# A small tile allotted 160 bytes more: the SBUF offset of every phase pool in a two-block transformer kernel

## The chip, the cores and the metric

The kernel runs on one core of one Trainium2 chip. The metric is the device time of one execution in microseconds; the runs shown are the median of three. One further execution was taken by the hardware profiler, and all views below are of that one.

## What is computed

Two transformer blocks on 256 tokens of width 2048, float32 throughout, one after the other. The first has a hybrid mixer (dilated attention, forgetting attention, gated linear attention), cross attention to 256 memory rows and a gated feed-forward with a short convolution; the second has a sparse attention, a gated delta rule, merge gates and a squared-ReLU feed-forward. Nearly all the work is in the products with the weights:

```python
def first_block(x, mem, ...):
    mem_n = rms_norm(mem, mem_norm)
    x = x + hybrid_mixer(rms_norm(x, norm_mix[l]), w_in[l], ..., w_out[l])
    x = x + memory_cross_attention(rms_norm(x, norm_cross[l]), mem_n, w_cq[l], w_ckv[l], w_co[l])
    x = x + conv_ffn(rms_norm(x, norm_ffn[l]), w_up[l], conv_w[l], conv_b[l], w_down[l])
    return rms_norm(x, norm_final)

def hybrid_layer(x, ...):                      # the second block
    proj = rms_norm_2(x, ln1_w) @ w_in
    ...
    x = x + (g_a * (o_a @ w_pa) + g_b * (o_b @ w_pb)) @ w_o
    h = rms_norm_2(x, ln2_w)
    return x + jnp.square(jax.nn.relu(h @ w_up)) @ w_down
```

## The kernel before

**Products.** A float32 product is made of three products of rounded parts. `chunk` (L327) brings 128x1024 weights from HBM by one transfer on SP's queue into a `raw` tile (four buffers), ScalarE rounds them into `hi`, VectorE takes the difference into `lo` (three buffers each); these tiles are in the pool "weights". Activations are kept the same way: a tile of 128x512 holds the rounded 256 columns and, behind them, the 256 columns of the rest. Such a tile is called `kt` where it comes from the pool "slots" (`new_kt`), `hk` where it comes from the pools "hidden1" and "hidden2" of the two feed-forwards, and `mkt` where it comes from the pool "late".

**Two forms.** `gemm_ws` (output tiles `ps_ws`, and `ps_pab` from `merged`) loads weights into TensorE's array and streams activations: each pair is 512 columns of `kt` over `hi` and 256 columns over `lo`. `gemm_as` (output tiles `ps_as`) loads 128 columns of an activation tile and streams 512 columns of weights, three matmuls a piece:

```python
def mm_as(o, kt, t, h, l, start, stop):
    xh, xl = kt[:, t * 128:t * 128 + 128], kt[:, 256 + t * 128:256 + t * 128 + 128]
    fill(o, xh, h, start, False)
    fill(o, xh, l, False, False)
    fill(o, xl, h, False, stop)
```

In the trace's names `ps_as<-hi,hk` is a matmul that streams `hi` over a loaded part of `hk`. All four down products of each feed-forward, and the product with `w_o` (from `mkt`), are of this form with tiles of the phase pools; `w_cv`, `w_v`, `w_out` and `w_co` are of this form with `kt` tiles of "slots". The rest of the large products are of the other form and stream `kt` tiles of "slots".

**Order.** A tile framework's scheduler lays down every engine's queue when the program is built, and allots SBUF. The long-lived pools come first, in the order const, weights, slots, norms, tiny; behind them are the pools of a phase, which `open_pools` opens and closes: "wide1", "held1", "work1" (mixer and cross attention), "hidden1", "work2" (first feed-forward), "gates" with "delta", then "wide2" and "heads", then "late" inside it (second block), "hidden2", "work4" (second feed-forward). The size of "tiny" thus sets where all of them begin.

**Places in SBUF** (byte offset in a partition, as the built program has them):

| tiles | pool | before | mod 512 |
|---|---|---|---|
| `raw`, `hi`, `lo` | weights | 24448 to 65408 | 384 |
| `kt` and other slots | slots | 67456 to 141184 | 384 |
| `pe` | tiny | 148064 | 96 |
| first phase tile | "wide1", "hidden1", "gates", "hidden2" | 149216 | 224 |
| `hk` | hidden1, hidden2 | from 149216, 2048 apart | 224 |
| `mkt` | late | from 171744, 2048 apart | 224 |
| tiles of "delta" behind the first padded tile | delta | from 175904 | 288 |

Of the kernel before, what the change touches and what calls it, by code (L numbers as in the profile page):

```python
# [225 lines left out]
def hybrid_blocks(ctx: ExitStack, tc: tile.TileContext, A: dict, out: bass.AP):  # L226
# [35 lines left out]
    def tiny(name, n, bufs=None):  # L262
        return tp.tile([128, n], F32, name=name, tag=name, bufs=bufs)
# [1056 lines left out]
    bias2 = []  # L1320
    for _ in bias_tiles(dtab2, bias2):
        pass
    pe = tiny("pe", 64, bufs=1)
    SP.dma_start(pe, A["pe"])
    w2c = wide("w2c", [128, 4, 128])
    SP.dma_start(w2c, A["cw2_2"].rearrange("p (a j) -> p a j", a=4))
# [275 lines left out]
```

## Time and profile before

| | |
|---|---|
| median of 3 runs | 2800.02 us (2799.59 to 2800.89) |
| profiled execution, device time | 2799.51 us |
| its span, first to last instruction | 2797.7 us |
| TensorE (PE) busy | 2765.9 us, 99% |
| weight loads into the array (PEld) | 2362.4 us, 84% |
| VectorE (DVE), ScalarE (ACT), GpSimd (POOL) busy | 65%, 49%, 6% |
| mean granted TensorE clock | 0.999 |

PE's busy time counts overlapping matmuls once, and a matmul's end is modelled, so a busy PE is not one at its peak. How fast the stream of matmuls runs is read from the starts of its rows in the timeline: a start belongs to the matmul itself, and the distance from one to the next is what one matmul costs when nothing is waited for. Rows of the timeline put neighbours of the same kind together (x2).

### The profile page before, as it was taken

The page shows a single profiled execution, that of the slowest core. Times are in us where ns is not written, and L with a number is a line of the kernel's source. Part 1 is how long each engine was busy: PE and PEld are TensorE (multiplying, and loading weights), DVE is VectorE, ACT ScalarE, POOL GpSimd, SP SyncE. Part 2 cuts the span into 40 slices and gives each one's busy share as a digit, 9 for nine tenths or more (in the row PEclk, how much of TensorE's full clock was granted, in tenths as well). Part 3 has the DMA queues.
Part 4 walks back from the last instruction along what each step waited for, and adds up shares of the span by engine and source line. Part 5 has one row for each costly group of instructions (what it writes and reads, how often), then busy time and mean ns, then how long its engine had stood idle before and what let it go on. Part 6 is the DMA issues. An engine that isn't in the chain of part 4 may idle for free.

```text
span 2797.7 us, 39304 instructions
## 1 busy us (share of the span) xinstructions
PE 2765.9 (99%) x14848; PEld 2362.4 (84%) x14848; DVE 1822.7 (65%) x2794; ACT 1379.1 (49%) x2230; POOL 169.4 (6%) x261
## 2 busy tenths in 40 slices
PE   7999999999999999999999999999999999999998
PEld 5988888888888888888889888888888888888887
DVE  7575675677764677657877767776656455565564
ACT  4545554544443444445555555555455344454453
POOL 5000000000000000000111010000100000000001
PEclk9999999999999999999999999999999999999999
DMA  6655446455555555565544448556666666666664
GB/s 214 184 173 176 144 146 203 159 187 192 185 185 187 188 188 184 182 209 184 179 151 149 152 143 255 171 151 185 188 202 192 185 191 188 188 190 188 189 188 158
DMA packets 148838, 507.28 MB, mean 181 GB/s; under 512 B 17036, under 2 KB 21672, under 8 KB 148648
## 3 DMA queue, kind: packets, MB, share of 16 engines
q1 hardware_dynamic: 148592, 504.74, 56.9%
q8 instruction: 116, 1.90, 0.3%
q14 instruction: 74, 0.61, 0.1%
q10 hardware_dynamic: 56, 0.04, 0.0%
HBM read 500.48 MB, written 4.23 MB: 180 GB/s over the span
## 4 chain that ended last, share of the span: by engine, by line
PE 96%; DVE 1%; ACT 1%; POOL 1%; DMA 1%; issue 0%; POOLq 0%; DVEq 0%; SPq 0%; ACTq 0%
PE ps_ws L272 51%; PE ps_as L272 34%; PE ps_pab L272 3%; PE ps_s L272 1%; PE ps_o L272 1%; PE ps_h L272 1%; PE ps_t L442 1%; PE ps_no L272 0%; PE ps_z L272 0%; PE ps_lv L272 0%; POOL mgate L1516 0%; DVE lo L337 0%; PE ps_y L272 0%; ACT hi L336 0%; DVE kt L404 0%
## 5 line engine op out<-in xcount | busy, mean ns | idle before, releaser
L337 DVE TENSOR_TENSOR lo<-raw,hi 128x1024 fp32r<-128x1024 f32 (+3 forms) x941 | 1144.7, 1218 | 785.2 <-ACT hi L336 777.8
L336 ACT CAST hi<-raw 128x1024 fp32r<-128x1024 f32 (+3 forms) x941 | 972.5, 1035 | 1051.9 <-PE ps_as L272 505.7
L272 PE MATMUL ps_ws<-kt,hi 128*128 128x512 f32 x4128 | 1466.0, 397 | 15.7 <-DVE kt L404 15.7
L272 PE MATMUL ps_ws<-kt,lo 128*128 128x256 f32 x4128 | 1173.3, 284 | 0.4 <-DVE lo L337 0.4
L272 PEld LDWEIGHTS ps_ws<-kt,hi 128*128 128x128 f32 x4128 | 778.3, 189 | 193.2 <-DVE kt L404 17.3
L272 PEld LDWEIGHTS ps_ws<-kt,lo 128*128 128x128 f32 x4128 | 784.0, 190 | 4.0 <-issue 2.6
L272 PE MATMUL ps_as<-hi,hk 128*128 128x512 f32 x1712 | 540.8, 396 | 0.0
L272 PEld LDWEIGHTS ps_as<-hi,hk 128*128 128x128 f32 x1712 | 322.5, 188 | 78.3
L272 PE MATMUL ps_as<-lo,hk 128*128 128x512 f32 x856 | 339.8, 397 | 0.0
L272 PE MATMUL ps_as<-hi,kt 128*128 128x512 f32 (+2 forms) x1024 | 295.2, 368 | 1.0 <-ACT hi L336 1.0
L272 PEld LDWEIGHTS ps_as<-hi,kt 128*128 128x128 f32 x1024 | 186.4, 188 | 26.6 <-ACT hi L336 1.4
L272 PEld LDWEIGHTS ps_as<-lo,hk 128*128 128x128 f32 x856 | 161.2, 188 | 38.8
L272 PE MATMUL ps_as<-lo,kt 128*128 128x512 f32 (+2 forms) x512 | 188.2, 368 | 0.9 <-DVE lo L337 0.9
L378 ACT COPY half<-ps_ws 128x256 f32<-128x256 f32 x258 | 95.0, 372 | 165.3 <-PE ps_ws L272 162.8
L379 DVE TENSOR_TENSOR half<-ps_ws,half 128x256 f32<-128x256 f32 x258 | 107.9, 421 | 63.6 <-ACT half L378 63.4
L272 PEld LDWEIGHTS ps_as<-lo,kt 128*128 128x128 f32 x512 | 96.3, 188 | 14.2 <-DVE lo L337 2.2
L272 PE MATMUL ps_pab<-kt,hi 128*128 128x512 f32 x256 | 91.3, 398 | 0.0
L272 PE MATMUL ps_as<-hi,mkt 128*128 128x512 f32 x256 | 82.1, 399 | 0.3 <-ACT hi L336 0.3
L272 PE MATMUL ps_pab<-kt,lo 128*128 128x256 f32 x256 | 72.9, 285 | 0.0
L272 PEld LDWEIGHTS ps_as<-hi,mkt 128*128 128x128 f32 x256 | 48.2, 188 | 12.1 <-issue 0.8
L272 PEld LDWEIGHTS ps_pab<-kt,hi 128*128 128x128 f32 x256 | 48.1, 188 | 11.1 <-DVE kt L401 0.2
L272 PE MATMUL ps_as<-lo,mkt 128*128 128x512 f32 x128 | 50.9, 398 | 0.3 <-DVE lo L337 0.3
(384 smaller groups left out, 1842.7 us busy)
## 6 DMA issues: line engine op xcount, KB each, us to landing
raw<-in_w_up SPq DMA_DIRECT2D x300, 512.0 KB, 3.6
raw<-in_w_dd SPq DMA_DIRECT2D x128, 512.0 KB, 3.7
raw<-in_w_dn SPq DMA_DIRECT2D x84, 512.0 KB, 4.3
raw<-in_w_m SPq DMA_DIRECT2D x64, 512.0 KB, 3.6
raw<-in_w_g SPq DMA_DIRECT2D x48, 512.0 KB, 3.3
raw<-in_w_qk SPq DMA_DIRECT2D x40, 512.0 KB, 3.3
raw<-in_w_v SPq DMA_DIRECT2D x32, 512.0 KB, 3.4
raw<-in_w_out SPq DMA_DIRECT2D x32, 512.0 KB, 3.3
```

What stands on the lines that cost most here:

```text
L272: return PE.matmul(o, l, r, start=start, stop=stop)
L336: ACT.copy(hi[:, a:b], raw[:, a:b])
L337: DVE.tensor_sub(lo[:, a:b], raw[:, a:b], hi[:, a:b])
L378: ACT.copy(s, ps[:, 256:512])
L379: DVE.tensor_tensor(s, ps[:, 0:256], s, op=ADD)
L442: PE.transpose(ps[:, t * 128:t * 128 + 128], x[:, c * 128:c * 128 + 128], ident)
```

## The change

The tile `pe`, which holds 64 float32 values a partition, is allotted 104 and used by its first 64: 416 bytes in place of 256. It is the tile before `kcc` and `H` in the pool "tiny", so these and every pool behind begin 160 bytes later: the first phase tile is at 149376 in place of 149216, which is 384 mod 512 in place of 224; `hk` and `mkt` are at 384 mod 512, the tiles of "delta" at 448. Weights, slots and norms stay where they are. On all five engines the queues hold the same instructions in the same order, with the same waits. A blank line is added ahead of L1323, so that lines behind it are one higher.

```diff
@@ -1320,7 +1320,8 @@
     bias2 = []
     for _ in bias_tiles(dtab2, bias2):
         pass
-    pe = tiny("pe", 64, bufs=1)
+
+    pe = tiny("pe", 104, bufs=1)[:, 0:64]
     SP.dma_start(pe, A["pe"])
```

## Rows read from the trace of the kernel before

**Rows 1.** The page: busy time, share, instructions; granted clock in 40 slices.

```profile
PE 2765.9 (99%) x14848; PEld 2362.4 (84%) x14848; DVE 1822.7 (65%) x2794; ACT 1379.1 (49%) x2230; POOL 169.4 (6%) x261
...
PEclk9999999999999999999999999999999999999999
```

**Rows 2.** The page: the chain that ended last, by engine.

```profile
PE 96%; DVE 1%; ACT 1%; POOL 1%; DMA 1%; issue 0%; POOLq 0%; DVEq 0%; SPq 0%; ACTq 0%
```

**Rows 3.** The page's groups: line, engine, operation, tiles, shape, count, busy us, mean ns.

```profile
L272 PE MATMUL ps_as<-hi,hk 128*128 128x512 f32 x1712 | 540.8, 396 | 0.0
...
L272 PE MATMUL ps_as<-lo,hk 128*128 128x512 f32 x856 | 339.8, 397 | 0.0
...
L272 PE MATMUL ps_as<-hi,mkt 128*128 128x512 f32 x256 | 82.1, 399 | 0.3 <-ACT hi L336 0.3
...
L272 PE MATMUL ps_as<-lo,mkt 128*128 128x512 f32 x128 | 50.9, 398 | 0.3 <-DVE lo L337 0.3
```

**Rows 4.** Timeline of PE, `hk` loaded: start us, duration us, instruction, count.

```profile
2169.82 0.39 PE L272 MATMUL ps_as<-lo,hk 128*128 128x512 f32 x1
...
2209.88 0.39 PE L272 MATMUL ps_as<-lo,hk 128*128 128x512 f32 x1
```

**Rows 5.** Timeline of PE, the same form with `kt` loaded.

```profile
212.07 0.39 PE L272 MATMUL ps_as<-lo,kt 128*128 128x512 f32 x1
...
251.51 0.39 PE L272 MATMUL ps_as<-lo,kt 128*128 128x512 f32 x1
```

**Rows 6.** Timeline of PE, the same form with `mkt` loaded.

```profile
2004.90 0.40 PE L272 MATMUL ps_as<-lo,mkt 128*128 128x512 f32 x1
...
2026.69 0.40 PE L272 MATMUL ps_as<-lo,mkt 128*128 128x512 f32 x1
```

**Rows 7.** Windows: stretch; busy us of PE, PEld, DVE, ACT, POOL; PEclk, DMA, GB/s.

```profile
212.00:252.00 40.00, 40.00 (x179) 33.11 (x178) 18.82 (x17) 17.81 (x22) 0.00 (x0) 1.00 0.56 194
2170.00:2210.00 40.00, 40.00 (x172) 32.14 (x172) 20.02 (x19) 14.87 (x15) 0.00 (x0) 1.00 0.61 188
```

**Rows 8.** Timeline of PE: `kt` loaded, just behind transposes that interrupt the stream.

```profile
454.19 0.60 PE L442 MATMUL ps_t<-cst,xs 128*128 128x128 f32 x4
...
454.87 0.40 PE L272 MATMUL ps_as<-lo,kt 128*128 128x512 f32 x1
...
456.96 0.39 PE L272 MATMUL ps_as<-lo,kt 128*128 128x512 f32 x1
...
457.64 0.39 PE L272 MATMUL ps_as<-lo,kt 128*128 128x512 f32 x1
```

**Rows 9.** Timeline of PE, pairs of the other form, second feed-forward.

```profile
2689.71 0.39 PE L272 MATMUL ps_ws<-kt,hi 128*128 128x512 f32 x1
...
2699.07 0.39 PE L272 MATMUL ps_ws<-kt,hi 128*128 128x512 f32 x1
```

**Rows 10.** Timeline of PE, the same pairs in the first feed-forward.

```profile
684.92 0.81 PE L272 MATMUL ps_tab<-ohr,tab 128*8 128x384 f32 x2
...
686.11 0.40 PE L272 MATMUL ps_ws<-kt,hi 128*128 128x512 f32 x1
...
693.88 0.40 PE L272 MATMUL ps_ws<-kt,hi 128*128 128x512 f32 x1
```

**Rows 11.** Groups of PE, 685.6 to 1171.2 us (first feed-forward).

```profile
L272 PE MATMUL ps_ws<-kt,hi 128*128 128x512 f32 x1024 | 362.0, 399 | 0.0
```

**Rows 12.** Groups of PE, 2073 to 2797 us (second feed-forward).

```profile
L272 PE MATMUL ps_ws<-kt,hi 128*128 128x512 f32 x1024 | 355.4, 391 | 0.0
```

**Rows 13.** Line L401, DVE: duration ns min/median/max, first and last start, forms.

```profile
L401 DVE TENSOR_TENSOR hk<-h,hk x64: 415/418/421, 2088.3 to 2704.7; 128x256 fp32r<-128x256 f32 x64
...
L401 DVE TENSOR_TENSOR kt<-gtmp,kt x8: 418/423/426, 1438.3 to 1676.9; 128x256 fp32r<-128x256 f32 x8
```

**Rows 14.** Groups by form: attention scores from work tiles, and from slots.

```profile
L272 PE MATMUL ps_s<-kpair,qpair 128*128 128x256 f32 x40 | 11.9, 379 | 0.0
...
L272 PE MATMUL ps_s<-ksw,nq 128*128 128x256 f32 x32 | 9.6, 380 | 0.0
```

## The prediction, made before the changed kernel ran

> **What bounds the kernel now.** I read the page's first part first: TensorE is busy for 2765.9 of 2797.7 us and its clock is granted in full, the 2.4 GHz level, in every slice [rows 1]. Then the chain of what ended last: 96% of it is TensorE's own [rows 2]. So there is hardly a wait to take away, and a change pays only if it alters how fast TensorE's stream of matmuls runs. The change removes, adds and moves no instruction; it moves tiles. The question is therefore whether a matmul's time depends on where its operands lie, and the trace can answer that, since it holds the same instruction with operands at different offsets.
>
> The form to look at is the one that loads part of an activation tile and streams 512 columns of weights. The streamed operand, `hi` or `lo`, always lies at 384 mod 512. The loaded one lies at 384 where it is a `kt` tile and at 224 where it is an `hk` or `mkt` tile. The busy column can't tell the rate, for matmuls overlap and each is shown for some 397 ns [rows 3]; the starts can:
>
> - `kt` loaded, 384: from 212.07 to 251.51 us there are 58 pieces of three matmuls, 39.44 us / 174 = 226.7 ns each [rows 5].
> - `hk` loaded, 224: from 2169.82 to 2209.88 us there are 57 pieces, 40.06 us / 171 = 234.3 ns each [rows 4].
> - `mkt` loaded, 224: from 2004.90 to 2026.69 us there are 31 pieces, 21.79 us / 93 = 234.3 ns each [rows 6].
>
> Nothing waits in these stretches. Side by side, equal windows of 40 us hold 179 matmuls with `kt` and 172 with `hk`, and what else goes on is much alike: VectorE busy 18.8 and 20.0 us, ScalarE 17.8 and 14.9 us, DMA 194 and 188 GB/s, clock 1.00 in both [rows 7]. The stretch with less ScalarE work and less DMA traffic is the slower one, so neither explains it. What is left as a visible difference is the place of the loaded operand.
>
> **The change part by part.** *The tile `pe`.* The extra 160 bytes are never written; the transfer into `pe` and the reads of it are as before. Cost: nothing.
>
> *`hk` and `mkt` go from 224 to 384 mod 512.* They are then placed to `hi` and `lo` as `kt` is. The page counts 1712 + 856 matmuls with `hk` and 256 + 128 with `mkt`, 2952 in all [rows 3]. If each goes from 234.3 to 226.7 ns, that is 2952 x 7.6 ns = 22.4 us. From this comes off what it takes to reach the lower rate. Behind transposes that interrupt a `kt` stream, nine matmuls take 2.09 us, 232.2 ns each, and the next three take 0.68 us, 226.7 ns each [rows 8]: 9 x 5.5 ns = 0.05 us for one start. By the code such stages are entered seven times (two parts of the first feed-forward, one product with `mkt`, four parts of the second), and the transposes of `to_kts` for four column blocks break into two of them, eight or nine times in all; 16 x 0.05 us = 0.8 us. So 21.6 us are saved.
>
> A rule speaks against this. First the rows: the same instruction with the same streamed operand took 226.7 or 234.3 ns [rows 4, 5]. The Trainium skill, "TensorE: Matmul & The Clock Gate", section "Step-by-step: what each phase is for", says that "Loading the next tile's weights doesn't steal SBUF read bandwidth from the running matmul", because the two operands have read ports of their own. By that rule the place of the loaded operand could not matter, and the sum would be nothing; by the rows it is 21.6 us. The trace does not agree with the rule, and I go by the rows.
>
> *What feeds the faster stream.* A chunk of 512 KB serves twelve such matmuls, 2.81 us at 234.3 ns and 2.72 us at 226.7 ns, so supply has to rise by 3%. In the `kt` window the same supply runs at 194 GB/s with VectorE under half busy, and no matmul waits [rows 7]. I cost it at nothing; if that cover failed, it would take back at most the 21.6 us.
>
> *The pairs of the other form.* Their operands, `kt` and weights, do not move. But they run at two rates with operands at the same offsets: in the second feed-forward 27 pairs take 9.36 us, 346.7 ns each [rows 9], in the first, behind a matmul of another kind, 22 pairs take 7.77 us, 353.2 ns each [rows 10]. So the rate also hangs on what ran before, and stays. The change alters what runs before them: an `hk` or `mkt` stage ends ahead of every part of the second feed-forward, and ahead of the second part of the first. Which rate each stretch then takes I can't read from the trace of before. The bounds are the two rates: 1024 pairs of the first feed-forward run slow [rows 11] and could gain 1024 x 6.5 ns = 6.7 us, 1024 of the second run fast [rows 12] and could lose 6.7 us. I take 0, the middle of the two, and keep both ends.
>
> *All other tiles of the phases* also move by 160 bytes. VectorE writes the rest of an `hk` tile in 418 ns and of a `kt` tile in 423 ns [rows 13], and the attention scores take 379 ns from tiles at 224 and 380 ns from slots at 384 [rows 14]. Neither shows a cost of the offset beyond 1%, the first engine is busy 65% of the time beside TensorE [rows 1], and the scores are 72 matmuls. A few tenths of a us either way; I take 0.
>
> *The sum.* The profiled execution took 2799.5 us, of which 2797.7 us is its span and 1.8 us lies around it. 2799.5 - 21.6 = 2777.9 us. The median of the runs is 0.5 us above the profiled one, so 2778.4 us; I give 2778 us.
>
> **The rivals.** *The stream only half follows.* With `hk` at 384 the matmuls stay at the rate that `kt` shows behind an interruption, 232.2 ns [rows 8], and never settle. Against it: every undisturbed `kt` stretch that I looked at settles at 226.7 ns. It gives 2952 x 2.1 ns = 6.2 us, 2794 us.
>
> *The offset is not the cause.* The `hk` and `mkt` tiles also lie higher in SBUF than all `kt` tiles, 149216 and up against 67456 to 141184. If the height and not the remainder sets the rate, a shift of 160 bytes changes nothing, and the time is 2800 us. For it: the trace has no loaded tile that is high and at 384, or low and at 224, in this form. Against it: `mkt` begins 22 KB above `hk` and runs at exactly its rate [rows 4, 6], so height would have to act as a step somewhere between 141 and 149 KB.
>
> *The place does not matter at all.* The two operands don't disturb each other, and something else that goes with the `hk` and `mkt` stages makes them slower, the same in three different stages of the program. Then too nothing changes, 2800 us. Against it stands that three matmuls after three take 0.70 us there whatever the other engines do, and never 0.68 [rows 4, 6, 7]. The rule of the Trainium skill quoted above, "TensorE: Matmul & The Clock Gate", is this case; the trace bears it out no further than that.
>
> *Slower: the second feed-forward's pairs fall to their slow rate.* The change shifts when each `hk` stage hands over to the pairs, the pairs keep the rate that they fall into, and all 1024 of them fall to 353.2 ns: 2800.0 + 6.7 = 2806.7 us, if the `hk` stages themselves gain nothing. Since they end on the same queue, it is slower by more than 0.2% only while the `hk` matmuls save less than 1.1 us in all, that is while they stay above 233.9 ns. If they settle, the same fall only moves the forecast to 2785 us. A collision of both operands at equal offsets would have to show in `kt` already; there the worst is 232.2 ns, below 234.3 [rows 4, 8].
>
> **How the numbers follow.** 0.2% of 2800 us is 5.6 us, about what a measurement of this kernel can tell from no change. The forecast, 2778 us with 2771 to 2785 by the pairs' two rates, has 0.76; the half-way case, 2794 us, 0.08; no effect, 2800 us, 0.06 by the height and 0.03 because the place does not matter, together 0.09; the slower one, 2807 us, 0.05; more gain than 2769 us, from pairs and other tiles together, 0.02. The range goes from 2769, 2 us below the pairs' lower end for the small tiles, to 2794, and so takes in the half-way case: 0.84. Faster by over 0.2%: 0.76 + 0.08 + 0.02 = 0.86; within 0.2%: 0.09; slower: 0.05.
>
> **What would show it.** In the timeline after, three matmuls on `hk` or `mkt` start 0.68 us after the three before them, not 0.70, and a window of 40 us in an `hk` stage holds 179, not 172. The `hk` groups' mean falls by some 7 ns. The stages' ends tell the rest: what the total has beyond 21.6 us must be found in the pairs, at 346.7 or 353.2 ns in each feed-forward. If `hk` stays at 0.70 us, the offset is not the cause; if it settles and the total does not follow, the pairs or the supply took it back, and either would show, as a rate or as idle time ahead of the `hk` matmuls.

## The result, and the profile after

The changed kernel takes 2781.76 us (2780.28 to 2784.14, four runs), the kernel before on the same chip 2799.81 us (2797.84 to 2800.89): the ratio of the two, from runs compared round by round, is 0.9941, 95% interval 0.9929 to 0.9954. That is 16.5 us; the two medians lie 18.1 us apart. The forecast was 2778 us, range 2769 to 2794. The profiled execution took 2780.28 us, its span 2778.5 us.

The page of the changed kernel, busy time first, then groups as in [rows 3]:

```profile
PE 2747.6 (99%) x14848; PEld 2359.8 (85%) x14848; DVE 1822.8 (66%) x2794; ACT 1378.6 (50%) x2230; POOL 168.7 (6%) x261
...
L272 PE MATMUL ps_as<-hi,hk 128*128 128x512 f32 x1712 | 528.1, 389 | 0.0
...
L272 PE MATMUL ps_as<-lo,hk 128*128 128x512 f32 x856 | 333.6, 390 | 0.0
...
L272 PE MATMUL ps_as<-hi,mkt 128*128 128x512 f32 x256 | 80.4, 392 | 0.3 <-ACT hi L336 0.3
...
L272 PE MATMUL ps_as<-lo,mkt 128*128 128x512 f32 x128 | 50.1, 391 | 0.6 <-DVE lo L337 0.6
```

The other engines are busy as long as before; only TensorE is 18.3 us less busy, at the same count. The `hk` and `mkt` groups have lost 7 ns of their mean, from 396 to 399 down to 389 to 392. Timeline of the changed kernel in the second feed-forward, `hk` loaded, to be held against [rows 4, 5]:

```profile
2159.62 0.39 PE L272 MATMUL ps_as<-lo,hk 128*128 128x512 f32 x1
...
2199.74 0.39 PE L272 MATMUL ps_as<-lo,hk 128*128 128x512 f32 x1
```

Between these lie 59 pieces of three matmuls: 40.12 us / 177 = 226.7 ns each, the rate of `kt` in [rows 5], where [rows 4] had 234.3 ns. The window over it, columns as in [rows 7], holds 179 matmuls in 40 us, as the `kt` window did, with DMA at 195 GB/s and nothing waiting:

```profile
2160.00:2200.00 40.00, 40.00 (x179) 33.10 (x178) 20.77 (x19) 15.05 (x15) 0.00 (x0) 1.00 0.65 195
```

The pairs of the other form changed as well, to the worse. Timeline of the changed kernel in the second part of the second feed-forward, behind an `hk` stage:

```profile
2240.41 0.40 PE L272 MATMUL ps_ws<-kt,hi 128*128 128x512 f32 x1
...
2249.25 0.40 PE L272 MATMUL ps_ws<-kt,hi 128*128 128x512 f32 x1
```

That is 25 pairs in 8.84 us, 353.6 ns each, where the second feed-forward's pairs ran at 346.7 ns before [rows 9]. The table gives the time by stages in both profiled executions, from the start of a stage's first matmul to that of the next stage's:

| stage | before, us | after, us | difference |
|---|---|---|---|
| first feed-forward, `hk`, part 0 | 123.69 | 119.71 | -3.98 |
| first feed-forward, `hk`, part 1 | 120.86 | 117.39 | -3.47 |
| `w_o` with `mkt` | 94.1 | 92.0 | -2.1 |
| second feed-forward, `hk`, four parts | 359.61 | 348.06 | -11.55 |
| second feed-forward, pairs, four parts | 356.36 | 361.58 | +5.22 |
| everything else | | | -3.8 |

Some of the last row has nothing to do with places. In the execution of the kernel before, TensorE's granted clock fell to half, the 1.2 GHz level, from 1776.3 to 1779.7 us, behind 3.5 us of matmuls of 16 columns. The slices of [rows 1] are 70 us long and hide it. Windows, columns as in [rows 7], of the kernel before and of the same stage in the changed kernel:

```profile
1776.30:1779.60 3.30, 3.30 (x12) 2.81 (x12) 0.42 (x1) 0.00 (x0) 0.00 (x0) 0.50 0.19 78
```

```profile
1766.80:1770.10 3.30, 3.30 (x21) 2.93 (x21) 1.31 (x4) 1.29 (x3) 0.00 (x0) 1.00 0.17 68
```

The kernel before lost 1.4 us there.

### The profile page after: what moved, and what is told of

It is laid out like the page before. It is cut to its first block, busy times and chain, and to the rows that moved or that the text cites. A ratio compares the mean times of both kernels' runs of the same rounds, so it can differ in the third digit from the quotient of the medians.

```text
span 2778.5 us, 39304 instructions
## 1 busy us (share of the span) xinstructions
PE 2747.6 (99%) x14848; PEld 2359.8 (85%) x14848; DVE 1822.8 (66%) x2794; ACT 1378.6 (50%) x2230; POOL 168.7 (6%) x261
## 4 chain that ended last, share of the span: by engine, by line
PE 96%; DVE 1%; ACT 1%; POOL 1%; issue 0%; DMA 0%; POOLq 0%; DVEq 0%; SPq 0%; ACTq 0%
PE ps_ws L272 52%; PE ps_as L272 34%; PE ps_pab L272 3%; PE ps_s L272 1%; PE ps_o L272 1%; PE ps_h L272 1%; PE ps_t L442 1%; PE ps_no L272 1%; PE ps_z L272 0%; PE ps_lv L272 0%; POOL mgate L1517 0%; DVE lo L337 0%; PE ps_y L272 0%; ACT hi L336 0%; DVE kt L404 0%
## 5 line engine op out<-in xcount | busy, mean ns | idle before, releaser
L272 PE MATMUL ps_ws<-kt,hi 128*128 128x512 f32 x4128 | 1467.6, 398 | 16.5 <-DVE kt L404 16.5
L272 PEld LDWEIGHTS ps_ws<-kt,hi 128*128 128x128 f32 x4128 | 777.5, 188 | 197.0 <-DVE kt L404 18.3
L272 PE MATMUL ps_as<-hi,hk 128*128 128x512 f32 x1712 | 528.1, 389 | 0.0
L272 PE MATMUL ps_as<-lo,hk 128*128 128x512 f32 x856 | 333.6, 390 | 0.0
```

What stands on the lines that cost most here:

```text
L272: return PE.matmul(o, l, r, start=start, stop=stop)
```

## The experiments

Two theories were open after the result. R: a matmul's rate hangs on the offset of the operand that is loaded, relative to that of the operand that is streamed. A: it hangs on the loaded operand's own alignment (224 is an odd multiple of 32, 384 a multiple of 128). The second question was why the pairs slowed.

**e1 and e2: eight offsets.** The 16 `hk` tiles of each part of the second feed-forward were put in four groups of four, each group behind a pad, here for e1; e2 has pads of 0, 24, 24 and 40 floats.

```diff
+                g = len(hk) // 4
+                if part == 0 and len(hk) % 4 == 0 and (8, 8, 16, 32)[g]:
+                    pad = hp.tile([128, (8, 8, 16, 32)[g]], F32, name="pad", tag=f"pad{g}", bufs=1)
+                    POOL.memset(pad, 0.0)
-                kt = hp.tile([128, 512], F32R, name="hk2", tag="hk2")
+                kt = hp.tile([128, 512], F32R, name=names[g], tag=names[g], bufs=8)
```

> The changed kernel, with the 16 activation tiles of each part of the second feed-forward in four groups of four at other offsets: hkp 32, hkq 64, hkr 128 and hks 256 bytes past 384 mod 512, that is at 416, 448, 0 and 128 mod 512. The streamed weights stay at 384. Each group gives 24 matmuls in a row, sixteen times over. Theory R, the rate is set by the loaded operand's offset relative to the streamed one's, and only 0 mod 512 is good: all four groups at 234 ns a matmul. Theory A, the loaded operand's own alignment sets it: if 64 bytes count, hkp at 234 ns and hkq, hkr, hks at 227 ns; if 128 bytes count, hkq at 234 ns too; if 512 less 128 counts, all four at 234 ns. Theory H, height in SBUF, is out already, since the change itself moved the rate.

> The same with the groups at 0 (hkp), 96 (hkq), 192 (hkr) and 352 (hks) bytes past 384 mod 512: at 384, 480, 64 and 224 mod 512. hks has the offset of the kernel before, hkp that of the change. Theory R: hkp 227 ns, hkq, hkr and hks 234 ns. Theory A with 64 bytes: hkp and hkr 227 ns, hkq and hks 234 ns; with 128 bytes: hkp alone 227 ns.

Timeline of e1, groups hkp (32 bytes past the weights) and hks (256):

```profile
2351.52 0.39 PE L272 MATMUL ps_as<-lo,hkp 128*128 128x512 f32 x1
...
2356.42 0.40 PE L272 MATMUL ps_as<-lo,hkp 128*128 128x512 f32 x1
```

```profile
2346.07 0.39 PE L272 MATMUL ps_as<-lo,hks 128*128 128x512 f32 x1
...
2350.83 0.39 PE L272 MATMUL ps_as<-lo,hks 128*128 128x512 f32 x1
```

Timeline of e2, groups hkr (192) and hks (352, the offset of the kernel before):

```profile
2363.48 0.40 PE L272 MATMUL ps_as<-lo,hkr 128*128 128x512 f32 x1
...
2368.29 0.39 PE L272 MATMUL ps_as<-lo,hkr 128*128 128x512 f32 x1
```

```profile
2346.80 0.40 PE L272 MATMUL ps_as<-lo,hks 128*128 128x512 f32 x1
...
2351.72 0.40 PE L272 MATMUL ps_as<-lo,hks 128*128 128x512 f32 x1
```

From a group's first such row to its eighth are seven pieces, 21 matmuls. All eight, worked out so:

| loaded less streamed, mod 512 | loaded at | seven pieces, us | ns a matmul |
|---|---|---|---|
| 0 | 384 | 4.76 | 226.7 |
| 32 | 416 | 4.90 | 233.3 |
| 64 | 448 | 4.90 | 233.3 |
| 96 | 480 | 4.92 | 234.3 |
| 128 | 0 | 4.88 | 232.4 |
| 192 | 64 | 4.81 | 229.0 |
| 256 | 128 | 4.76 | 226.7 |
| 352 | 224 | 4.92 | 234.3 |

Theory A falls in all its forms: a tile at 0 mod 512, as well aligned as can be, is slow, one at 64 mod 512 is faster than that, and one at 128 is as fast as one at 384. Theory R is left, to be held against the tile's own offset in e3, but its expectation that only 0 is good was wrong: 256 is as good, and 192 lies between. The two runs are single ones of 2786.72 and 2787.24 us; their verdict rests on the rows, not on their times.

**e3: everything 32 bytes further, the relation kept.**

```diff
-    nhalf = const("nhalf", [128, 16])
+    nhalf = const("nhalf", [128, 24])[:, 0:16]
```

> The changed kernel with one long-lived small tile allotted 32 bytes more, ahead of the weights' pool: weights, slots and phase tiles all lie at 416 mod 512, the relation between them as in the change. Theory R: hk, mkt and kt loaded stay at 226.7 ns, the total at 2782 us but for the pairs' rates (up to 7 us either way). Theory A (64 or 128 bytes): all 2952 matmuls with hk and mkt go back to 234.3 ns, +22 us, and the 960 of 512 columns with kt as well, +7 us: 2811 us.

2783.69 us, 0.9951 (0.9936 to 0.9966). Timeline of e3, `hk` loaded, now at 416 mod 512 under weights at 416:

```profile
2160.00 0.39 PE L272 MATMUL ps_as<-lo,hk 128*128 128x512 f32 x1
...
2199.44 0.39 PE L272 MATMUL ps_as<-lo,hk 128*128 128x512 f32 x1
```

58 pieces in 39.44 us, 226.7 ns. The same 416 under weights at 384 gave 233.3 ns in e1. So at the same own offset the relation decides. The total is R's, not the 2811 us of A. The tiles `raw`, `hi` and `lo` all share one offset, so the runs can't tell the streamed tile from its neighbours in the pool as the partner; but three matmuls on `hk` take 0.70 to 0.71 us all through [rows 4], whatever the engines that fill those tiles do.

**e4: the second feed-forward's tiles back at 224.**

```diff
     hp, kp = open_pools(("hidden2", 32), ("work4", 2))
+    POOL.memset(hp.tile([128, 88], F32, name="pad", tag="pad", bufs=1), 0.0)
```

> The changed kernel with a pad of 352 bytes ahead of the tiles of the second feed-forward alone, which puts its hk tiles back to 224 mod 512; the first feed-forward and mkt keep the change. Own theory: the 1536 matmuls with hk there go from 226.7 back to 234.3 ns, +11.7 us, and the pairs behind them, which the settled stream had handed over in the slow rate, 768 of them, return to 346.7 ns, -5.1 us: 2788 us. Rival, the pairs' rate has nothing to do with how the hk stage ahead of them ran (it came with the pairs' own place in the program): they stay at 353.3 ns, 2793 us.

2788.17 us, 0.9969 (0.9956 to 0.9981): the number of its own theory. Timeline of e4, an `hk` stage and the pairs behind it:

```profile
2159.61 0.40 PE L272 MATMUL ps_as<-lo,hk 128*128 128x512 f32 x1
...
2199.67 0.40 PE L272 MATMUL ps_as<-lo,hk 128*128 128x512 f32 x1
```

```profile
2250.63 0.39 PE L272 MATMUL ps_ws<-kt,hi 128*128 128x512 f32 x1
...
2259.99 0.39 PE L272 MATMUL ps_ws<-kt,hi 128*128 128x512 f32 x1
```

57 pieces in 40.06 us, 234.3 ns again; and 27 pairs in 9.36 us, 346.7 ns again. The pairs' slow rate came with the offset of the `hk` stage ahead of them, not with their own operands, which did not move.

The rate of the last `hk` matmuls does not decide it by itself. In e2 the last group ahead of the pairs is hks, at the offset of the kernel before. Timeline of e2, the end of that group and the pairs behind it:

```profile
2236.27 0.39 PE L272 MATMUL ps_as<-lo,hks 128*128 128x512 f32 x1
...
2239.08 0.40 PE L272 MATMUL ps_as<-lo,hks 128*128 128x512 f32 x1
...
2239.89 0.40 PE L272 MATMUL ps_ws<-kt,hi 128*128 128x512 f32 x1
...
2249.78 0.40 PE L272 MATMUL ps_ws<-kt,hi 128*128 128x512 f32 x1
```

Four pieces in 2.81 us, 234.2 ns, and yet 28 pairs in 9.89 us, 353.2 ns. So a hand-over from the slow `hk` rate can lead to the slow pairs as well; what in a hand-over leads to which rate no run shows.

**e5: another hand-over.** `gemm_ws` gets a number of leading steps whose four matmuls run 512, 512, 256, 256 columns in place of 512, 256, 512, 256. The work is the same.

```diff
+                if k < swap:
+                    for t in range(2):
+                        fill(ps[t], hi[:, s[t]], kts[k], k == 0, False)
+                    for t in range(2):
+                        fill(ps[t][:, 0:256], lo[:, s[t]], kts[k][:, 0:256], False, k == n - 1)
+                else: ...
-            ps = gemm_ws(kts, A["w_up"][i])
+            ps = gemm_ws(kts, A["w_up"][i], swap={11: 1, 22: 16}.get(i, 0))
-            ps = gemm_ws(kts, A["w_up2"][part * 8 + u])
+            ps = gemm_ws(kts, A["w_up2"][part * 8 + u], swap=(16, 0 if u else 1, 0 if u else 2, 1)[part])
```

> The changed kernel with another order of the first matmuls of some stages that stream kt, so that the pairs are met in another phase: a swapped step is two of 512 columns and then two of 256 in place of 512, 256, 512, 256. First feed-forward: one step swapped at i = 11 (just behind the bias table's matmul), sixteen at i = 22 (entry of its second part). Second feed-forward: part 0 all steps swapped, part 1 one step at its entry, part 2 two steps at its entry, part 3 one step at the start of each of its eight products. Own theory, the pairs have two steady rates at the same offsets and keep the one that the phase at hand-over leads to: at least one of the four entries that ran at 353.3 ns in the changed kernel (from i = 11; i = 22; parts 1 and 2) goes to 346.7 ns and stays there, each worth 1.7 us (parts 1, 2), 2.3 us (from i = 11) or 4.5 us (i = 22); the total falls by 2 to 10 us. Rival, the rate belongs to the place in the program (which slots the kt tiles have, what the other engines do there): no entry changes, total 2782 us.

2774.89 us, 0.9918 (0.9902 to 0.9935). Part 3 of the second feed-forward has one swapped step at the start of each of its eight products of 32 pairs. Timeline of e5, the swapped steps of products 2, 4, 5 and 6, seen as two `hi` in a row (those of products 1 and 3 start at 2589.00 and 2611.39 us):

```profile
2600.29 0.63 PE L272 MATMUL ps_ws<-kt,hi 128*128 128x512 f32 x2
...
2622.68 0.63 PE L272 MATMUL ps_ws<-kt,hi 128*128 128x512 f32 x2
...
2633.78 0.63 PE L272 MATMUL ps_ws<-kt,hi 128*128 128x512 f32 x2
...
2645.07 0.63 PE L272 MATMUL ps_ws<-kt,hi 128*128 128x512 f32 x2
```

The products take 11.29, 11.10, 11.29, 11.10 and 11.29 us in turn: 352.8 and 346.9 ns a pair. Behind the first, each swapped step flips the rate, and between them it stays. At the entries one swapped step left the pairs slow (part 1, and i = 11, where it ran right behind the bias table's matmul), two made them fast (part 2), and so did sixteen (i = 22). Part 0, with all its steps swapped, ran at 348.3 ns a pair, slower than the 346.7 ns that it has in the changed kernel. The rival, that the rate belongs to the place in the program, falls. The expectation "at least one of four" was met by two.

**e6: slots 256 bytes from the weights.**

```diff
-        s = wp.tile([128, 256], F32, name="half", tag="half", bufs=2)
+        s = wp.tile([128, 288], F32, name="half", tag="half", bufs=2)[:, 0:256]
-        early, v, r = tiny("early", 1), ...
+        early, v, r = tiny("early", 1, bufs=1), ...
```

> The kernel before with a pad of 256 bytes behind the weights' pool and 96 bytes taken from the tiny pool: the slots (kt) lie at 128 mod 512, 256 bytes from the weights, hk and mkt at 384, as in the change. In the sweep a loaded operand 256 bytes from the streamed one ran at 226.7 ns from its first matmuls on, without the nine slower ones. Theory R2, two operands 256 apart are as good as 0 apart and settle at once: the interrupted kt stages of the mixer save about a us in all, and the pairs (weights loaded, kt streamed, now 256 apart) lose their slow rate and run at 346.7 ns everywhere: some 2000 pairs of the changed kernel at 353.3 ns would save 13 us, 2768 us. Rival, the pairs keep both rates at any offset, by their own phase: within 7 us of 2782 us either way. Against both: the pairs run slower than 353.3 ns, over 2789 us.

2783.48 us, 0.9948 (0.9933 to 0.9962): the number of the rival in which the pairs keep both rates. Timeline of e6, pairs in the second and in the first feed-forward:

```profile
2249.75 0.40 PE L272 MATMUL ps_ws<-kt,hi 128*128 128x512 f32 x1
...
2259.64 0.40 PE L272 MATMUL ps_ws<-kt,hi 128*128 128x512 f32 x1
```

```profile
569.69 0.39 PE L272 MATMUL ps_ws<-kt,hi 128*128 128x512 f32 x1
...
579.75 0.39 PE L272 MATMUL ps_ws<-kt,hi 128*128 128x512 f32 x1
```

28 pairs in 9.89 us and 29 in 10.06 us: 353.2 and 346.9 ns, the same two rates at 256 as at 0. `kt` loaded ran at 226.7 ns (56 pieces in 38.08 us), but behind transposes it still needed six matmuls to settle, as many as in the changed kernel at 0, not none. The hope drawn from the sweep was wrong.

**e7: flipping only the slow stretches.** The changed kernel with one swapped step at i = 12, two at i = 22, two at the entry of parts 1 to 3, one at the twelfth merge gate.

```diff
-            ps = gemm_ws(kts, A["w_up"][i])
+            ps = gemm_ws(kts, A["w_up"][i], swap={12: 1, 22: 2}.get(i, 0))
-            ps = gemm_ws(kts, A["w_up2"][part * 8 + u])
+            ps = gemm_ws(kts, A["w_up2"][part * 8 + u], swap=2 if part and u == 0 else 0)
-        ps = gemm_ws(kts, A["w_m"][c])
+        ps = gemm_ws(kts, A["w_m"][c], swap=1 if c == 11 else 0)
```

> The changed kernel with swapped steps (two of 512 columns, then two of 256) only where a stretch of pairs ran slow and only as many as flip it by the run before: one at i = 12 and two at i = 22 in the first feed-forward, two at the entry of parts 1, 2 and 3 of the second, one at the start of the twelfth merge gate. Own theory, the rate is a state that a swapped step flips and that else stays: 320 pairs from i = 12, some 670 from i = 22, 768 in parts 1 to 3 and some 290 in the merges go from 353.3 to 346.7 ns: 2.1 + 4.4 + 5.1 + 1.9 = 13.5 us off the changed kernel's 2782 us, 2768 us. Rival, the flips seen were chance of one execution: some stretches stay slow, 2772 to 2780 us, and the three parts, which are alike, come out unlike.

2769.86 us (2768.88 to 2772.06), 0.9898 (0.9881 to 0.9914): better than both kernels, its interval clear of the changed kernel's. Timeline of e7, entry of part 1, where the changed kernel ran at 353.6 ns:

```profile
2232.73 0.62 PE L272 MATMUL ps_ws<-kt,hi 128*128 128x512 f32 x2
...
2235.85 0.39 PE L272 MATMUL ps_ws<-kt,hi 128*128 128x512 f32 x1
...
2244.87 0.39 PE L272 MATMUL ps_ws<-kt,hi 128*128 128x512 f32 x1
```

26 pairs in 9.02 us, 346.9 ns, and parts 2 and 3 alike; so do the pairs from i = 12 and from i = 22. The merges stayed slow. Right behind the step come three transposes, of which the last row below is the first, and across such interruptions a rate need not last: in the changed kernel the merges' pairs ran at 346.7 ns from 1770 to 1775 us and at 353.3 ns from 1858 us on.

```profile
1847.46 0.64 PE L272 MATMUL ps_ws<-kt,hi 128*128 128x512 f32 x2
1847.94 0.40 PE L272 MATMUL ps_ws<-kt,lo 128*128 128x256 f32 x2
1848.17 0.27 PE L538 MATMUL ps_pt<-cst,sneg 128*128 128x128 f32 x1
```

Without the 1.9 us of the merges the expectation was 2770 us.

That the merges were slow is not a matter of places either. Up to the second feed-forward the kernels of e1 and e2 are the same, with the same matmuls in the same order on tiles at the same places. Timelines of the merges, first of e1, then of e2:

```profile
1858.69 0.40 PE L272 MATMUL ps_ws<-kt,hi 128*128 128x512 f32 x1
...
1867.01 0.39 PE L272 MATMUL ps_ws<-kt,hi 128*128 128x512 f32 x1
```

```profile
1858.05 0.40 PE L272 MATMUL ps_ws<-kt,hi 128*128 128x512 f32 x1
...
1866.52 0.40 PE L272 MATMUL ps_ws<-kt,hi 128*128 128x512 f32 x1
```

24 pairs take 8.32 us in e1, 346.7 ns each, and 8.47 us in e2, 352.9 ns each. Behind interrupted streams the rate thus differs from one execution to the next.

**e8: slots 64 bytes from the weights.** `half` is allotted 264 floats in place of 256 and `pe` 88, so that `kt` lies 64 bytes past the weights' offset and `hk` and `mkt` at it.

```diff
-        s = wp.tile([128, 256], F32, name="half", tag="half", bufs=2)
+        s = wp.tile([128, 264], F32, name="half", tag="half", bufs=2)[:, 0:256]
-    pe = tiny("pe", 64, bufs=1)
+    pe = tiny("pe", 88, bufs=1)[:, 0:64]
```

> The kernel before with the slots (kt) moved to 64 bytes past the weights' offset (448 mod 512) and hk and mkt to 384, as in the change. Theory R: kt loaded under streamed weights goes from 226.7 to 233 ns, as hkq did in the sweep; hk and mkt stay at 226.7 ns. For the pairs (weights loaded, kt streamed), if relation counts there as well, their rates are no more 346.7 and 353.3 ns but higher. Rival, the pairs don't depend on the offset at all: 346.7 and 353.3 ns as before. Total, by kt alone, 960 x 6.5 ns = 6 us over the changed kernel, 2788 us.

One run of 2786.76 us. Timeline of e8, `kt` loaded, then pairs behind an `hk` stage:

```profile
212.06 0.40 PE L272 MATMUL ps_as<-lo,kt 128*128 128x512 f32 x1
...
249.86 0.40 PE L272 MATMUL ps_as<-lo,kt 128*128 128x512 f32 x1
```

```profile
2249.90 0.39 PE L272 MATMUL ps_ws<-kt,hi 128*128 128x512 f32 x1
...
2259.67 0.39 PE L272 MATMUL ps_ws<-kt,hi 128*128 128x512 f32 x1
```

54 pieces in 37.80 us: `kt` went from 226.7 to 233.3 ns, the sweep's number for 64. With that the other half of the comparison of [rows 4, 5] is shown too: now `kt` is the slow tile and `hk` the fast one. The pairs took 28 in 9.77 us, 348.9 ns, a rate that the same order of matmuls shows at no other offset, and 353.6 ns in the part before (28 in 9.90 us). So the pairs depend on the relation as well, by 2 ns in their fast rate; this rests on one execution.

## Why the prediction was right

*The `hk` and `mkt` matmuls.* Forecast 226.7 ns for 234.3 and 21.6 us with the settling taken off; the seven stages together gained 3.98 + 3.47 + 2.1 + 11.55 = 21.1 us. The cause named, the place of the loaded operand and not the stage, is shown by e4 (224 put back in one feed-forward brings 234.3 ns back there), by e8 (`kt` made slow) and by e3 (the relation, not the offset). The rivals of the height and of no dependence fall with the result itself, and the half-way one with 226.7 ns in place of 232.2. What makes the relation count no run shows.

*The rule that spoke against it.* The Trainium skill, "TensorE: Matmul & The Clock Gate", section "Step-by-step: what each phase is for", says that loading the next tile's weights takes no SBUF read bandwidth from the running matmul. If that were all, the place of the loaded operand would make no difference. The runs show one of up to 7.6 ns in 234.3, by the offset alone; the measurement decides.

*The supply.* It kept up: 195 GB/s and no wait in the window after.

*The pairs.* This term was mis-sized. I took 0 between the bounds of 6.7 us either way; it measured +5.2 us in the second feed-forward and nothing in the first. Three of four parts there fell to the slow rate, all three behind an `hk` stage. That mechanism, a shifted hand-over whose rate lasts, was the one of the slower rival, which had the whole of it at +6.7 us; e4, e5 and e7 show it: undone with the offset, flipped by one swapped step within a stretch or two at an entry, and worth 12 us when put right, first feed-forward included. Why this hand-over leads to the slow rate stays open (e2).

*All other tiles.* Taken as 0, it measured -3.8 us, but little of that can be put down to the tiles. The 1.4 us of the clock's fall at 1776 us do not follow the places: in e3, e4, e6 and e8, where tiles had moved as well, the clock fell in the same stage, and in the changed kernel, e1, e2, e5 and e7 it did not. So the prediction's reading of a clock granted in full in every slice was true of the slices only. Another 0.6 us is one longer wait of TensorE for VectorE at 1346 us, some 1.1 us lies in the first 53 us, and 0.8 us in small pieces between 225 and 485 us, where the streams are interrupted. The four runs of the changed kernel themselves spread by 3.9 us, and e1 and e2 show that the pairs' rate in interrupted stages changes with the execution. Whether any of the rest is the offset of other tiles stays open.

*The sum.* -21.1 + 5.2 - 3.8 = -19.7 us between first and last matmul; the span shrank by 19.2 us, the medians by 18.1 us. The forecast of 2778 us missed by 3.8 us. That it came so close is in part luck: two terms taken at nothing, +5.2 and -3.8 us, largely cancel in the profiled executions. The 21 us of the `hk` and `mkt` matmuls are no luck.

## What to carry to other kernels

Where TensorE is the bound and nothing waits, look at the starts of its matmuls: the same shape at two distances is time that no view of waits shows. Try to place the operand that is loaded at the offset of the operand that is streamed, mod 512 bytes, or 256 bytes from it (both ran at 226.7 ns here); a few bytes in a small tile ahead of the pools can do it, and any later change of a pool's size can undo it. Then look at the stretches of one form for two steady rates, and try another order of a few matmuls where one stretch hands over to the next. Before two profiled executions are compared stage by stage, look for a fall of the clock that is shorter than a slice.

## What the runs showed of the hardware

- A stream of 512-column matmuls with a load each ran at 226.7 ns a matmul when both operands lay 0 or 256 bytes apart mod 512, at 229.0 ns at 192, and at 232.4 to 234.3 ns at 32, 64, 96, 128 and 352, at a granted clock of 1.00.
- Pairs of 512 and 256 columns had two steady rates at the same offsets, 346.7 and 353.3 ns or so, at 0 and at 256 bytes; at 64 bytes they had 348.9 and 353.3. A rate lasts for hundreds of pairs. Behind an interruption by other matmuls it can come out either way, between two executions of the same matmuls too (e1 and e2). Within a stretch, one step in the order 512, 512, 256, 256 flips it (e5). What the two states are, no run shows.
